# Low parts of the run-ahead chunks by an adding DMA, one-hots in groups of two, and 39 chunks ahead dealt sooner

## The chip, the cores and the metric

The kernel runs on one core of a Trainium2 chip. The metric is the time of one execution on the device in microseconds (us). Before the change three runs gave a median of 1723.9 us (1723.31 to 1724.44). In what follows PE is the matmul engine (TensorE), PEld its weight loads, DVE is VectorE, ACT is ScalarE, POOL is GpSimd, and SP only issues DMAs.

## The reference

One transformer-like layer on 512 tokens of width 1024, in float32. First a token-mixing half (two kinds of attention, gates, projections, a residual add). Then a retrieval half, which is what the change touches:

```
q = rms_norm(x) @ w_q                          # 8 heads, two halves of 128 each
scores = q . sub_keys                          # 128 keys per half
top 16 of each half, sums of pairs, top 16     # -> 16 experts per head, of 128*128
gate = softmax(best)
act = gelu(u[expert] . h)                      # u, v: 16384 experts x 1024
out = x + sum(gate * act * v[expert])
```

An expert's number is 128 times one key index plus another. 8 heads with 16 experts make 128 experts for each token.

## The kernel before

**The dense way.** For three of the four blocks of 128 tokens (`DT`, together 384 tokens) the kernel doesn't gather rows of `u` and `v`. It runs over all 128 *chunks* of 128 experts. For a chunk `first` (L678) computes the products of `u` with all 384 tokens on PE (`pa`) and their gelu (`ga`); the sweep (L799) multiplies `ga` by a gate matrix that is zero where an expert wasn't chosen, and adds its product with the chunk of `v` into `acc`. The fourth block (`GT`) gathers its rows with indirect DMAs from POOL (L762) and multiplies them on DVE, in the background of the sweep.

**Two parts of a float.** PE multiplies a rounded format (`fp32r`). So each operand is split into a high part (rounded) and a low part (the rest), and `mm3` (L145) makes three matmuls: high by high, high by low, low by high. `split` (L668) makes the parts of a chunk in two halves of 128x512: ACT copies to `uh` (L673), and an engine subtracts `uh` from the raw chunk `ut` into `ul` (L674). That engine is POOL for the chunks that run ahead, and DVE in the sweep. Each of `uh` and `ul` has three buffers (`UB`), so three halves are in flight; a chunk is 24 matmuls, 12 for a half.

**Running ahead.** `AHEAD` = 37 chunks of `first` run before the sweep. `more` (L692) deals them out: 2 at once, then one at every third step of `retrieve` (L638, called for the four blocks, 6 steps each), then one for each group of 16 tokens in the gate stage below, and the rest.

**Retrieval.** For each block, `retrieve` turns the chosen places into key indices: ACT copies the places to a one-hot tile `oh` (L646), DVE compares (L647), multiplies by the candidates' indices (L649), and adds up the 16 columns in a tree of four additions of 8, 4, 2 and 1 columns (L651 to L653).

**The gate stage.** For each of 24 groups of 16 tokens (`TB`), DVE builds five tiles of 128x2048 two-byte numbers: one-hots of both key indices (`o1`, `o2`), multiplied by parts of the gate (L738 to L742). In these tiles `TI` = 4 tokens lie side by side: element (key, token) of a group of four stands at 4*key + token. PE multiplies for each token the 128x128 one-hots of both sides, twice (32 matmuls in a group, L747). So the 128 columns that such a matmul reads stand 4 elements, or 8 bytes, apart. ACT copies the result out of PSUM (L750, L751), and SP stores it to DRAM (`spool`).

**Order.** A scheduler puts the instructions of each engine in an order when the program is built; on the chip each engine runs its list in that order and waits at the first that isn't ready. Buffers are released by semaphores when the last reader is done.

Of the kernel before, what the change touches and what calls it, by code (L numbers as in the profile page):

```python
# [8 lines left out]
F32 = mybir.dt.float32  # L9
F32R = mybir.dt.float32r  # L10
# [4 lines left out]
AF = mybir.ActivationFunctionType  # L15
OP = mybir.AluOpType
AX = mybir.AxisListType
# [12 lines left out]
RES = 8  # L30
OCT = 8
TB = 16
TI = 4
AHEAD = 37
S2, GAT, WB, UB, VB = 8, 4, 3, 3, 3
COLS = 3 * 3 * D
PACE = 1.05 * 2 * P * len(GT) / (COLS * (2 * P - AHEAD))
# [10 lines left out]
def block_kernel(ctx, tc, x, mix_gain, w_in, gate_bias, q_gain, k_gain, sinks, w_up_a, w_up_b, w_out,  # L48
                 ffn_gain, w_q, keys_t, peer_u, peer_v, peer_ut, out):
    nc = tc.nc  # L50
# [587 lines left out]
    def retrieve(j):  # L638

        r = NT - 1 - j  # L640
        ia, ib = (gwk.tile([P, HEADS, 16], F32, name=f"{n}{j}") if j in DT else
                  rp.tile([P, HEADS, 16], F32, name=f"{n}{j}") for n in ("ia", "ib"))
        for sel, half, dst in ((a_, 0, ia), (b_, 1, ib)):
            oh = rp.tile([P, HEADS, 16, 16], BF16, name="oh", tag="oh", bufs=2)
            oh2 = oh.rearrange("p h k j -> p (h k) j")
            A.activation(oh2, sel[:, r, :, None].to_broadcast([P, P, 16]), AF.Copy)  # L646
            V.tensor_tensor(out=oh2, in0=oh2, in1=i16[:, None, :].to_broadcast([P, P, 16]), op=OP.is_equal)  # L647
            yield
            V.tensor_tensor(out=oh, in0=oh, in1=idf[:, r, :, half, None, :].to_broadcast([P, HEADS, 16, 16]), op=OP.mult)  # L649
            yield  # L650
            for n in (8, 4, 2):  # L651
                V.tensor_tensor(out=oh[:, :, :, 0:n], in0=oh[:, :, :, 0:n], in1=oh[:, :, :, n:2 * n], op=OP.add)  # L652
            V.tensor_tensor(out=dst, in0=oh[:, :, :, 0], in1=oh[:, :, :, 1], op=OP.add)  # L653
            yield
        KEYS[j] = ia, ib, gate[:, r]
        if j in GT:
            ROWS[j] = gwk.tile([P, HEADS, 16], I32, name=f"ex{j}")
            V.scalar_tensor_tensor(out=ROWS[j], in0=ib, scalar=128.0, in1=ia, op0=OP.mult, op1=OP.add)
# [9 lines left out]
    def split(pool, src, name, eng, bufs):  # L668

        res = []  # L670
        for b in range(2):
            hi, lo = (pool.tile([P, KD // 2, P], F32R, name=name + n, tag=name + n, bufs=bufs) for n in ("h", "l"))
            A.activation(hi, src[:, 4 * b:4 * b + 4], AF.Copy)  # L673
            eng.tensor_tensor(out=lo, in0=src[:, 4 * b:4 * b + 4], in1=hi.bitcast(F32), op=OP.subtract)  # L674
            res.append((hi, lo))
        return res

    def first(i2, eng=G):  # L678

        ut = us.tile([P, KD, P], F32, name="ut", tag="ut", bufs=2)  # L680
        nc.sync.dma_start(ut, peer_ut[i2])
        u = split(us, ut, "u", eng, UB)
        pa = pa_.tile([P, 512], F32, name="pa", tag="pa")
        for k in range(KD):
            mm3(pa[:, :T], u[k // 4], h2T, (SL, k % 4, SL), (SL, k, slice(0, T)), k == 0, k == KD - 1)
        ga = upool.tile([P, T], F32, name="ga", tag="ga", bufs=AHEAD)
        A.activation(ga, pa[:, :T], AF.Gelu)
        return ga
# [3 lines left out]
    def more(n):  # L692
        for i2 in range(len(ahead), min(len(ahead) + n, AHEAD)):
            ahead[i2] = first(i2)

    more(2)
    for j in DT + GT:
        for i, _ in enumerate(retrieve(j)):
            if i % 3 == 0:
                more(1)  # L700
    ret.close()

# [1 line left out]
    with ExitStack() as st:  # L704
        bw = scope(st, "bw")
        pg = scope(st, "pg", 4, space=PSUM)
        rep = bw.tile([P, P, TI], F16, name="rep")
        G.iota(rep, pattern=[[1, P], [0, TI]], base=0, channel_multiplier=0, allow_small_or_imprecise_dtypes=True)
        oh = [P, TB // TI, P, TI]
        keys = rep[:, None].to_broadcast(oh)  # L710

        def spread(t):
            return t.rearrange("p (q i) -> p q i", i=TI)[:, :, None, :].to_broadcast(oh)

        for j in DT:
            pt = pg.tile([P, 4, P], F32, name="pg", tag="pg")
            for i in range(3):
                nc.tensor.transpose(pt[:, i, :], KEYS[j][i].rearrange("p h k -> p (h k)"), ident)
            sel = bw.tile([P, 2, P], F16, name="sel", tag="sel")
            A.activation(sel, pt[:, 0:2, :], AF.Copy)  # L720

            part = bw.tile([P, 2, P], F16, name="part", tag="part")
            two, man = (bw.tile([P, P], F32, name=n, tag=n) for n in ("two", "man"))
            power = bw.tile([P, P], BF16, name="power", tag="power")
            V.tensor_scalar(two.bitcast(I32), pt[:, 2, :].bitcast(I32), 0x7F800000, None, op0=OP.bitwise_and)
            V.tensor_scalar(man.bitcast(I32), pt[:, 2, :].bitcast(I32), 0x007FFFFF, 0x3F800000, op0=OP.bitwise_and,
                            op1=OP.bitwise_or)
            V.tensor_copy(power, two)
            V.tensor_copy(part[:, 0, :], man)
            V.tensor_tensor(out=part[:, 1, :], in0=man, in1=part[:, 0, :], op=OP.subtract)  # L730
            for tb in range(P // TB):
                tg = (NT - 1 - j) * (P // TB) + tb
                ts = slice(tb * TB, (tb + 1) * TB)
                stage = bw.tile([P, SP, TB], F32, name="stage", tag="stage", bufs=2)
                o1 = bw.tile(oh, BF16, name="o1", tag="o1", bufs=2)
                o2 = bw.tile(oh, F16, name="o2", tag="o2", bufs=2)
                ow = bw.tile([P, 2, *oh[1:]], F16, name="ow", tag="ow", bufs=2)
                V.tensor_tensor(out=o2, in0=keys, in1=spread(sel[:, 1, ts]), op=OP.is_equal)  # L738
                for i in range(2):
                    V.tensor_tensor(out=ow[:, i], in0=o2, in1=spread(part[:, i, ts]), op=OP.mult)  # L740
                V.tensor_tensor(out=o1, in0=keys, in1=spread(sel[:, 0, ts]), op=OP.is_equal)
                V.tensor_tensor(out=o1, in0=o1, in1=spread(power[:, ts]), op=OP.mult)  # L742
                for q in range(TB // TI):
                    pp = pg.tile([P, TI, P], F32, name="pg", tag="pg")
                    for i in range(TI):
                        for s in range(2):
                            nc.tensor.matmul(pp[:, i, :], lhsT=o1[:, q, :, i], rhs=ow[:, s, q, :, i],  # L747
                                             start=(s == 0), stop=(s == 1))
                    c0 = tg * TB + 4 * q
                    A.activation(gres[:, :, c0:c0 + 4], pp[:, :, 0:RES].rearrange("p t i -> p i t"), AF.Copy)  # L750
                    A.activation(stage[:, :, 4 * q:4 * q + 4], pp[:, :, RES:P].rearrange("p t i -> p i t"), AF.Copy)  # L751
                more(1)
                nc.sync.dma_start(spool[:, :, tg].rearrange("o p i t -> p o i t"),
                                  stage.rearrange("p (o i) t -> p o i t", i=OCT))
# [44 lines left out]
    for i2 in range(P):  # L799
        ga = ahead.pop(i2)  # L800
        vt = vpool.tile([P, KD, P], F32, name="vt", tag="vt", bufs=3)
        nc.sync.dma_start(vt.rearrange("p k n -> p (k n)"), peer_v[i2 * P:(i2 + 1) * P, :])
        v = [[t.rearrange("p k n -> p (k n)") for t in half] for half in split(vpool, vt, "v", V, VB)]
        if i2 >= RES and (i2 - RES) % OCT == 0:
            gs = vpool.tile([P, T // TB, OCT, TB], F32, name="gs", tag="gs")
            nc.sync.dma_start(gs, spool[(i2 - RES) // OCT])
        wh = vpool.tile([P, T], F32R, name="wh", tag="wh")
        wl = vpool.tile([P, T], F32R, name="wl", tag="wl")
        if i2 < RES:
            V.tensor_tensor(out=ga, in0=ga, in1=gres[:, i2, :], op=OP.mult)  # L810
        else:
            g3 = ga.rearrange("p (b t) -> p b t", t=TB)
            V.tensor_tensor(out=g3, in0=g3, in1=gs[:, :, (i2 - RES) % OCT, :], op=OP.mult)
        A.activation(wh, ga, AF.Copy)
        V.tensor_tensor(out=wl, in0=ga, in1=wh.bitcast(F32), op=OP.subtract)
        if i2 + AHEAD < P:
            ahead[i2 + AHEAD] = first(i2 + AHEAD, V)
        for b in range(2):
            for j in DT:
                mm3(acc[j][:, 512 * b:512 * b + 512], (wh, wl), v[b], (SL, cols(NT - 1 - j)), (SL, SL), i2 == 0, i2 == P - 1)  # L820
# [44 lines left out]
```

## Time and profile before

| | |
|---|---|
| median of 3 runs | 1723.9 us |
| the profiled execution: time, span | 1720.6 us, 1718.9 us |
| PE busy | 1651.5 us, 96% of the span |
| DVE, ACT, POOL busy | 75%, 43%, 34% |
| first `pa`, first gate matmul, first `acc`, last `acc` start | 510.6, 604.6, 810.9, 1711.6 us |

The span runs from the first to the last instruction; 1.7 us of the profiled time lie around it. A matmul's duration includes its way through the array, and matmuls overlap; so PE's rate is read from the distance of two starts, not from durations, and a busy share of 96% is not 96% of what PE can do.

### The profile page before, as it was taken

To read this page: it belongs to the slowest core of one execution; us is meant where nothing else is said; L and a number is where in the kernel's file an instruction comes from. 1 tells how busy PE (TensorE), PEld (TensorE's weight loads), DVE (VectorE), ACT (ScalarE), POOL (GpSimd) and SP (SyncE) were. 2 spreads that over 40 slices of the span, in tenths; PEclk is the share of its full clock that TensorE was granted. 3 is DMA by queue.
4 is the path that set the end of the run, shared out by engine and by line. 5 is a ranking of instruction groups with operands and counts; after the bars stand their busy time and mean duration, and the time that the engine had idled before them with its cause. 6 is when DMAs were issued, how large, how long until landed. Compare 5 with 4: busy or idle time off the path is not lost.

```text
span 1718.9 us, 24631 instructions
## 1 busy us (share of the span) xinstructions
PE 1651.5 (96%) x8969; PEld 1466.4 (85%) x8969; DVE 1282.0 (75%) x2471; ACT 745.8 (43%) x1457; POOL 582.7 (34%) x446
## 2 busy tenths in 40 slices
PE   6999999999996899989999999999999999999998
PEld 5887777798885798989999999999999999998886
DVE  5444345635999998898897878777777777877874
ACT  4557635533324454545344343343344434443442
POOL 4100011512323654453343434334444343433310
PEclk9999999999998899999999999999999999999999
DMA  4321231123301364657999988888988888877874
GB/s 159 98 75 50 73 89 59 62 87 125 108 1 62 107 205 145 208 171 244 406 372 344 323 277 314 319 290 318 322 281 313 316 295 310 290 269 248 294 234 145
DMA packets 158347, 361.29 MB, mean 210 GB/s; under 512 B 10385, under 2 KB 86161, under 8 KB 156305
## 3 DMA queue, kind: packets, MB, share of 16 engines
q1 hardware_dynamic: 120496, 224.94, 37.5%
q0 software_dynamic: 36864, 134.23, 23.5%
q8 instruction: 70, 1.15, 0.3%
q10 hardware_dynamic: 864, 0.54, 0.1%
q14 instruction: 53, 0.43, 0.1%
HBM read 331.89 MB, written 27.26 MB: 209 GB/s over the span
## 4 chain that ended last, share of the span: by engine, by line
PE 81%; DVE 13%; issue 3%; ACT 1%; POOL 1%; DMA 0%; DVEq 0%; SPq 0%; ACTq 0%; POOLq 0%
PE acc L148 10%; PE acc L150 10%; PE acc L149 10%; PE pa L148 9%; PE pa L150 9%; PE pa L149 9%; PE pg L747 5%; PE mm L149 5%; PE mm L150 5%; PE mm L148 5%; DVE tt L566 1%; PE z L462 1%; DVE oh L652 1%; PE mm L490 1%; DVE idx L568 1%
## 5 line engine op out<-in xcount | busy, mean ns | idle before, releaser
L148 PE MATMUL pa<-h2Th,uh 128*128 128x384 f32 x1024 | 349.3, 341 | 17.6 <-ACT uh L673 17.2
L150 PE MATMUL pa<-h2Th,ul 128*128 128x384 f32 x1024 | 349.6, 341 | 6.8 <-POOL ul L674 6.8
L149 PE MATMUL pa<-h2Tl,uh 128*128 128x384 f32 x1024 | 348.3, 340 | 0.0
L673 ACT ACTIVATE uh<-ut 128x512 fp32r<-128x512 f32 x256 | 160.9, 632 | 323.4 <-PE pa L149 237.1
L148 PE MATMUL acc<-vh,wh 128*128 128x512 f32 x768 | 301.1, 392 | 0.0
L150 PE MATMUL acc<-vh,wl 128*128 128x512 f32 x768 | 299.9, 390 | 0.0
L149 PE MATMUL acc<-vl,wh 128*128 128x512 f32 x768 | 298.6, 389 | 0.0
L762 POOL DMA_INDIRECT row<-peer_u,ex x128 | 175.2, 1369 | 250.0 <-DVE row L774 193.8
L762 POOL DMA_INDIRECT row<-peer_v,ex x128 | 166.5, 1301 | 267.4 <-DVE xg L784 193.0
L673 ACT ACTIVATE vh<-vt 128x512 fp32r<-128x512 f32 x256 | 159.8, 624 | 140.3 <-PE acc L150 136.5
L148 PEld LDWEIGHTS pa<-h2Th,uh 128*128 128x128 f32 x1024 | 195.6, 191 | 23.5 <-ACT uh L673 19.0
L150 PEld LDWEIGHTS pa<-h2Th,ul 128*128 128x128 f32 x1024 | 195.3, 191 | 8.8 <-POOL ul L674 8.8
L149 PEld LDWEIGHTS pa<-h2Tl,uh 128*128 128x128 f32 x1024 | 195.3, 191 | 3.7
L674 POOL TENSOR_TENSOR ul<-ut,uh 128x512 fp32r<-128x512 f32 x74 | 137.0, 1860 | 172.4 <-ACT uh L673 165.4
L674 DVE TENSOR_TENSOR vl<-vt,vh 128x512 fp32r<-128x512 f32 x256 | 176.6, 690 | 23.5 <-ACT vh L673 22.0
L674 DVE TENSOR_TENSOR ul<-ut,uh 128x512 fp32r<-128x512 f32 x182 | 125.5, 690 | 85.4 <-ACT uh L673 85.4
L150 PEld LDWEIGHTS acc<-vh,wl 128*128 128x128 f32 x768 | 144.1, 188 | 32.5
L149 PEld LDWEIGHTS acc<-vl,wh 128*128 128x128 f32 x768 | 144.2, 188 | 27.3
L148 PEld LDWEIGHTS acc<-vh,wh 128*128 128x128 f32 x768 | 144.2, 188 | 26.3
L784 DVE SCALAR_TENSOR_TENSOR xg<-row,wt,xg 128x1024 f32<-128x1024 f32 x128 | 163.7, 1279 | 1.3
L774 DVE SCALAR_TENSOR_TENSOR row<-row,h 128x1024 f32<-128x1024 f32 x128 | 151.4, 1219 | 4.8 <-DMA row<-peer_u,ex 4.7
L158 DVE TENSOR_TENSOR wlo<-w,whi 128x1024 fp32r<-128x1024 f32 x52 | 64.9, 1250 | 85.9 <-ACT whi L157 81.7
(232 smaller groups left out, 2823.5 us busy)
## 6 DMA issues: line engine op xcount, KB each, us to landing
ut<-peer_ut SPq DMA_DIRECT2D x128, 512.0 KB, 4.9
vt<-peer_v SPq DMA_DIRECT2D x128, 512.0 KB, 6.9
spool<-stage SPq DMA_DIRECT2D x24, 960.0 KB, 5.0
gs<-spool SPq DMA_DIRECT2D x15, 1536.0 KB, 9.7
w<-w_in SPq DMA_DIRECT2D x17, 1024.0 KB, 5.4
w<-w_q SPq DMA_DIRECT2D x8, 1024.0 KB, 5.6
w<-w_out SPq DMA_DIRECT2D x4, 1024.0 KB, 5.1
x<-x SPq DMA_DIRECT2D x4, 512.0 KB, 5.8
```

What stands on the lines that cost most here:

```text
L148: nc.tensor.matmul(ps, lhsT=l[0][li], rhs=r[0][ri], start=start, stop=False)
L149: nc.tensor.matmul(ps, lhsT=l[0][li], rhs=r[1][ri], start=False, stop=False)
L150: nc.tensor.matmul(ps, lhsT=l[1][li], rhs=r[0][ri], start=False, stop=stop)
L158: eng.tensor_tensor(out=lo, in0=raw, in1=hi.bitcast(F32), op=OP.subtract))
L462: nc.tensor.matmul(z[:, :nk], lhsT=qT[:, h, cols(NT - 1 - j)], rhs=kbT[:, h // 2, row0(j):S], start=True, stop=True)
L490: nc.tensor.matmul(PY[j][s * 64:(s + 1) * 64, h // 2, :], lhsT=vb[:, NT - 1 - j + b, h * DH:(h + 1) * DH], rhs=lt[:, b, :], start=(b == 0) ...
L673: A.activation(hi, src[:, 4 * b:4 * b + 4], AF.Copy)
L674: eng.tensor_tensor(out=lo, in0=src[:, 4 * b:4 * b + 4], in1=hi.bitcast(F32), op=OP.subtract)
L747: nc.tensor.matmul(pp[:, i, :], lhsT=o1[:, q, :, i], rhs=ow[:, s, q, :, i], start=(s == 0), stop=(s == 1))
L762: G.indirect_dma_start(out=t, out_offset=None, in_=src, in_offset=bass.IndirectOffsetOnAxis(ap=ex[:, h, k:k + 1], axis=0))
L774: V.scalar_tensor_tensor(out=t, in0=t, scalar=1.0, in1=h2, op0=OP.mult, op1=OP.mult, accum_out=wt[:, h, k:k + 1]))
L784: V.scalar_tensor_tensor(out=xj, in0=t, scalar=wt[:, h, k:k + 1], in1=xj, op0=OP.mult, op1=OP.add))
```

## The change

The low part of a run-ahead chunk is made in another way (`split_dma`): ACT first writes minus the rounded chunk into `ul`, then POOL issues a DMA that reads the same half chunk from DRAM again and adds it on to `ul`; ACT then writes `uh` as before. The chunks that are made in the sweep keep the subtraction on DVE. `TI` becomes 2, with the group of four tokens in PSUM kept. `AHEAD` becomes 39; 5 chunks are dealt at once, and one at every second step of `retrieve`. The tree of four additions in `retrieve` becomes one `tensor_reduce`.

```diff
-TI = 4
-AHEAD = 37
+TI = 2
+AHEAD = 39
@@ retrieve
-            for n in (8, 4, 2):
-                V.tensor_tensor(out=oh[:, :, :, 0:n], in0=oh[:, :, :, 0:n], in1=oh[:, :, :, n:2 * n], op=OP.add)
-            V.tensor_tensor(out=dst, in0=oh[:, :, :, 0], in1=oh[:, :, :, 1], op=OP.add)
+            V.tensor_reduce(out=dst, in_=oh, axis=AX.X, op=OP.add)
@@ new
+    def split_dma(pool, src, raw, name, bufs):
+
+        res = []
+        for b in range(2):
+            hi, lo = (pool.tile([P, KD // 2, P], F32R, name=name + n, tag=name + n, bufs=bufs) for n in ("h", "l"))
+            k = slice(4 * b, 4 * b + 4)
+            A.activation(lo, src[:, k], AF.Copy, scale=-1.0)
+            G.dma_start(lo, raw[:, k], accum_op=OP.add)
+            A.activation(hi, src[:, k], AF.Copy)
+            res.append((hi, lo))
+        return res
@@ first
-        u = split(us, ut, "u", eng, UB)
+        u = split(us, ut, "u", V, UB) if sweep else split_dma(us, ut, peer_ut[i2], "u", UB)
@@
-    more(2)
+    more(5)
     for j in DT + GT:
         for i, _ in enumerate(retrieve(j)):
-            if i % 3 == 0:
+            if i % 2 == 0:
                 more(1)
@@ gate stage
-                for q in range(TB // TI):
-                    pp = pg.tile([P, TI, P], F32, name="pg", tag="pg")
-                    for i in range(TI):
+                for q in range(TB // 4):
+                    pp = pg.tile([P, 4, P], F32, name="pg", tag="pg")
+                    for i in range(4):
+                        t, k = divmod(4 * q + i, TI)
                         for s in range(2):
-                            nc.tensor.matmul(pp[:, i, :], lhsT=o1[:, q, :, i], rhs=ow[:, s, q, :, i],
+                            nc.tensor.matmul(pp[:, i, :], lhsT=o1[:, t, :, k], rhs=ow[:, s, t, :, k],
                                              start=(s == 0), stop=(s == 1))
```

What the scheduler makes of it on POOL, from the run-ahead chunks on. Before (`ul` the low parts, `wlo` low parts of the weights of w_q, `row` the first gathers of the sweep):

```order
L158 TENSOR_TENSOR wlo<-w,whi 128x1024 x13
L674 TENSOR_TENSOR ul<-ut,uh 128x512 x21
L708 IOTA rep 128x512
L674 TENSOR_TENSOR ul<-ut,uh 128x512
L762 DMA row<-peer_u,ex_5512 128x1024
L674 TENSOR_TENSOR ul<-ut,uh 128x512
```

And after it:

```order
L158 TENSOR_TENSOR wlo<-w,whi 128x1024 x13
L683 DMA ul<-peer_ut 128x512 x23
L718 IOTA rep 128x256
L773 DMA row<-peer_u,ex_5781 128x1024
L683 DMA ul<-peer_ut 128x512
L773 DMA row<-peer_u,ex_5781 128x1024
L683 DMA ul<-peer_ut 128x512 x2
```

POOL's 74 subtractions become 78 DMA issues in the same places of its list; it has no other work between the last `wlo` and the gathers.

On ACT, in the stretch in which `retrieve` runs; `oh` are the copies that `retrieve` needs, `ga` the gelu of a chunk. Before:

```order
L646 ACTIVATE oh<-b__5053 128x2048
L687 ACTIVATE ga<-pa 128x384
L673 ACTIVATE uh<-ut 128x512 x3
L646 ACTIVATE oh<-a__5052 128x2048
L687 ACTIVATE ga<-pa 128x384
L646 ACTIVATE oh<-b__5053 128x2048
```

And after it:

```order
L646 ACTIVATE oh<-b__5053 128x2048
L682 ACTIVATE ul<-ut 128x512
L684 ACTIVATE uh<-ut 128x512
L646 ACTIVATE oh<-a__5052 128x2048
L697 ACTIVATE ga<-pa 128x384
L682 ACTIVATE ul<-ut 128x512
L684 ACTIVATE uh<-ut 128x512
L682 ACTIVATE ul<-ut 128x512
L684 ACTIVATE uh<-ut 128x512
L646 ACTIVATE oh<-b__5053 128x2048
```

The negated copy stands ahead of the high part of the same half, and one or two halves now stand between two `oh` copies. On PE's list 318 `pa` matmuls (13 1/4 chunks) stand ahead of the first gate matmul before the change, and 408 (17 chunks) after it.

In the gate stage, one round on ACT between the evictions of two groups. Before:

```order
L750 ACTIVATE gres<-pg 128x8x4
L751 ACTIVATE stage<-pg 128x120x4
L673 ACTIVATE uh<-ut 128x512
L687 ACTIVATE ga<-pa 128x384
L673 ACTIVATE uh<-ut 128x512
L750 ACTIVATE gres<-pg 128x8x4
```

And after it:

```order
L761 ACTIVATE gres<-pg 128x8x4
L762 ACTIVATE stage<-pg 128x120x4
L682 ACTIVATE ul<-ut 128x512
L684 ACTIVATE uh<-ut 128x512
L682 ACTIVATE ul<-ut 128x512
L684 ACTIVATE uh<-ut 128x512
L697 ACTIVATE ga<-pa 128x384
L761 ACTIVATE gres<-pg 128x8x4
```

Both halves of a chunk are now made between two evictions, so the DMAs of a chunk can't be issued before the last eviction of the group ahead; PE's list has one group of 32 gate matmuls and one chunk in turn.

## Rows read from the trace of the kernel before

**Rows 1.** Page: busy us and instructions; engines in the chain that ended last
```profile
PE 1651.5 (96%) x8969; PEld 1466.4 (85%) x8969; DVE 1282.0 (75%) x2471; ACT 745.8 (43%) x1457; POOL 582.7 (34%) x446
...
PE 81%; DVE 13%; issue 3%; ACT 1%; POOL 1%; DMA 0%; DVEq 0%; SPq 0%; ACTq 0%; POOLq 0%
```
**Rows 2.** Busy time by stage: stretch, its length, engines, clock, DMA share, GB/s
```profile
511.00:605.00 94.00, 66.10 (x325) 61.47 (x324) 91.11 (x230) 40.01 (x53) 50.10 (x30) 0.85 0.27 84
605.00:811.00 206.00, 196.70 (x1367) 191.63 (x1366) 185.34 (x142) 104.37 (x270) 93.56 (x49) 0.95 0.63 189
811.00:1557.00 746.00, 746.00 (x3783) 679.25 (x3782) 602.14 (x928) 296.99 (x550) 300.74 (x223) 1.00 0.88 315
1557.00:1712.00 155.00, 154.96 (x684) 127.97 (x682) 106.00 (x143) 61.62 (x110) 31.75 (x28) 1.00 0.70 231
```
**Rows 3.** First and last start us, by tile: pa, gate matmuls, acc (durations ns min/median/max)
```profile
L148 PE MATMUL pa<-h2Th,uh x1024: 335/336/686, 510.6 to 1556.2; 128*128 128x384 f32 x171
...
L747 PEld LDWEIGHTS <-o x768: 111/117/138, 604.6 to 797.3; 128*128 128x128 bf16 x192
L747 PE MATMUL pg<-ow,o x768: 287/297/303, 604.6 to 797.4; 128*128 128x128 f16 x192
...
L150 PE MATMUL acc<-vh,wl x768: 388/389/397, 811.4 to 1711.6; 128*128 128x512 f32 x192
```
**Rows 4.** Waits from 605 to 811 us: who, for whom, us, times, longest
```profile
PE pg L747 <- DVE o L742: 9.3, 2, 5.3
```
**Rows 5.** Timeline of PE: start us, us; 384 columns first and last of 20, then a gate block
```profile
631.61 0.34 PE L148 MATMUL pa<-h2Th,uh 128*128 128x384 f32 x1
...
634.90 0.34 PE L149 MATMUL pa<-h2Tl,uh 128*128 128x384 f32 x1
635.08 3.95 PE L747 MATMUL pg<-ow,o 128*128 128x128 f16 x32
```
**Rows 6.** Timeline of PE with 256 columns, first and last of 7, and their weight loads
```profile
366.26 0.28 PE L150 MATMUL mm<-whi,mgl 128*128 128x256 f32 x1
...
366.98 0.28 PE L150 MATMUL mm<-whi,mgl 128*128 128x256 f32 x1
...
366.26 0.19 PEld L148 LDWEIGHTS mm<-whi,mgh 128*128 128x128 f32 x1
```
**Rows 7.** Timeline of PE: eight transposes in a row
```profile
395.90 1.04 PE L549 MATMUL tp<-ident,h 128*128 128x128 f32 x8
```
**Rows 8.** A 2048-element build on DVE, alone and beside a subtraction on POOL
```profile
L738 DVE TENSOR_TENSOR o<-rep,sel x24: 1206/1210/2279, 594.2 to 783.5; 128x2048 f16<-128x2048 f16 x24
...
640.87 4.21 POOL L674 TENSOR_TENSOR ul<-ut,uh 128x512 fp32r<-128x512 f32 x2 [3.66 <-ACT uh L673]
...
641.62 2.32 DVE L740 TENSOR_TENSOR ow<-o,part 128x2048 f16<-128x2048 f16 x1
```
**Rows 9.** The tree's narrow steps (timeline), and a reduction over 512 elements
```profile
563.53 0.42 DVE L653 TENSOR_TENSOR ia<-oh 128x128 f32<-128x128 bf16 x1
563.87 0.44 DVE L652 TENSOR_TENSOR oh<-oh 128x256 bf16<-128x256 bf16 x1
...
L614 DVE TENSOR_REDUCE gsum<-gate x1: 677/677/677, 536.7 to 536.7; 128x32 f32<-128x512 f32 x1
```
**Rows 10.** ACT: copies and evictions, 605 to 811 us (mean ns); retrieval's copy
```profile
L751 ACT ACTIVATE stage<-pg 128x480 f32<-128x480 f32 x96 | 54.4, 567 | 0.0
L673 ACT ACTIVATE uh<-ut 128x512 fp32r<-128x512 f32 x48 | 30.4, 633 | 43.2 <-PE pa L149 28.0 <-issue 8.1 <-POOL ul L674 4.5
L750 ACT ACTIVATE gres<-pg 128x32 f32<-128x32 f32 x96 | 18.9, 197 | 57.6 <-PE pg L747 57.5
L687 ACT ACTIVATE ga<-pa 128x384 f32<-128x384 f32 x24 | 11.4, 476 | 0.0
...
L646 ACT ACTIVATE oh<-b__5053 x4: 1898/1899/1902, 541.8 to 579.9; 128x2048 bf16<-128x2048 bf16 x4
```
**Rows 11.** POOL's gathers of 512 KB, 585 to 830 us: issue ns, and landing
```profile
L762 POOL DMA_INDIRECT row<-peer_u,ex x11: 933/1678/1967, 593.9 to 825.6; - x11
...
DMA to landing us min/median/max: 4.4/6.6/11.9
```

More of the change, by code (lines that the diff above doesn't have):

```diff
@@ L676, in split, with first @@
         return res
-    def first(i2, eng=G):
+    def split_dma(pool, src, raw, name, bufs):
[8 more added lines that the diff above has]
+        return res
+    def first(i2, sweep=False):
         ut = us.tile([P, KD, P], F32, name="ut", tag="ut", bufs=2)
         nc.sync.dma_start(ut, peer_ut[i2])
-        u = split(us, ut, "u", eng, UB)
+        u = split(us, ut, "u", V, UB) if sweep else split_dma(us, ut, peer_ut[i2], "u", UB)
         pa = pa_.tile([P, 512], F32, name="pa", tag="pa")
@@ L816, in block_kernel @@
         if i2 + AHEAD < P:
-            ahead[i2 + AHEAD] = first(i2 + AHEAD, V)
+            ahead[i2 + AHEAD] = first(i2 + AHEAD, True)
         for b in range(2):
```

## The prediction

> **What bounds the kernel now.** I read the page's busy shares and its chain first [rows 1]: PE is busy 96% of the span and holds 81% of the chain, DVE 13%. Such a share hides pace, so I went on to the busy time by stage [rows 2]. The reader is to see there three stages. From 811 us on, in the sweep, PE is busy all of 746 us and all but 0.04 us of the last 155: what PE has to do there is all that counts. From 605 to 811, the gate stage, PE is idle for 206 - 196.7 = 9.3 us, all of it two waits for the one-hot builds [rows 4]. From 511 to 605, the retrieval, PE is busy for 66 of 94 us, at a mean granted clock of 0.85 of 2.4 GHz: the only hole of any size. The first and last starts [rows 3] give the frame: first chunk 510.6, first gate matmul 604.6, last `acc` matmul 1711.6.
>
> So there are two ways to win: PE work put into the hole, and PE work made shorter. Moving a chunk from the sweep to before it is worth nothing in itself, since PE does the same 128 chunks; two more chunks ahead count only where they stand in the hole.
>
> **PE's prices.** Starts, not durations. Twenty matmuls of 384 columns start from 631.61 to 634.90 [rows 5]: 3.29/19 = 173 ns each, so a half of 12 is 2.08 us and a chunk of 24 is 4.15 us. Seven of 256 columns start 0.72 us apart from first to last [rows 6]: 120 ns. 128 columns more thus cost 53 ns, and 128 columns alone would cost 120 - 53 = 67 ns. The gate block has 32 matmuls of 128 columns in 3.95 us; less one duration of 0.297 us, that is 3.65/31 = 118 ns [rows 3, 5], nearly twice 67. It isn't the weight loads: those of 0.19 us follow each other every 120 ns in rows 6, and the gate block's take 0.117 us [rows 3]. What sets the gate matmuls apart is that their columns stand 8 bytes apart in SBUF.
>
> **The change part by part.**
>
> *TI = 2.* The columns stand 4 bytes apart, as in the fp32r matmuls that run at full pace. Bounds: 118 ns (no gain) and 67 ns. I take 67, the price that the contiguous rows give: 768 x 51 ns = -39.2 us. On DVE the builds keep their 2048 elements; one alone takes 1.21 us [rows 8]. Their second operand now repeats pairs instead of fours. Bounds are 1.21 us and the 2.32 us that the same build takes beside POOL; I take 1.21, as a pair still is one 4-byte word, and price the other end as a rival.
>
> A rule speaks against the gain: the Trainium skill's page "SBUF — State Buffer", section "Door 1: The DMA port swizzle", says that SBUF is read in 16-byte lines and that two hits in a line are enough for full bandwidth. At 8 bytes a line has two hits, so by that rule nothing is gained here; the sum would be 1721 (first rival). The 118 ns of rows 5 against 67 speak against it, unless something else makes them slow.
>
> *Low parts by DMA.* It removes 74 subtractions on POOL. Beside them a build takes up to 2.32 us in place of 1.21 [rows 8], and DVE is busy 185 of 206 us in the gate stage [rows 2]. Without them five builds cost 5 x 1.21 = 6.05 us a group, 145 us in 24 groups. It adds on ACT 78 copies of 0.633 us (the negated parts), and on POOL 78 DMA issues. A group with a chunk then has on ACT 4 x (0.197 + 0.567) + 4 x 0.633 + 0.476 = 6.06 us [rows 10]: beside PE's work, if a round is longer than that. What matters is the time L from POOL's issue to the landing, because `ul` has three buffers. The trace has no adding DMA. Nearest are the gathers of 512 KB from the same queue: landing 4.4 us at least, 6.6 in the median, 11.9 at most [rows 11]. The new DMA writes half of that, but reads both the source and what it adds to. I take L = 5.0, near the gathers' lower end, for the bytes; the ends I keep are 3.7 (an estimate: the 4.4 less an issue's difference and half the transfer) and 11.9.
>
> The Trainium skill's page "DMA: Bandwidth & Descriptors", section "Anatomy of one DMA — SWDGE (gpsimd) path", has 2.0 us plus the bytes over 436 GB/s, about 2.6 us for 256 KB; it says nothing of adding. By it the sum would be about 1654.
>
> *The hole with 17 chunks.* On PE's list 17 chunks stand ahead of the first gate matmul, 13 1/4 before. A buffer's round is: half chunk 2.08, negated copy 0.63, DMA 5.0, three hand-overs about 0.4 = 8.1 us, for three halves at a time. Three halves are made early, and the last of 34 is the first of the twelfth round: 510.6 + 11 x 8.1 + 2.08 = 601.8. The eight copies of 1.9 us that `retrieve` needs [rows 10] now stand among these copies on ACT; I add all, 15.2 us: 617. So the first gate matmul comes 617 - 604.6 = 12.4 us later, with 3.75 chunks more done, 15.6 us of PE. Queued behind a `ul` that waits for its buffer are, on ACT, those copies (DVE waits for them) and gelus; on POOL only further low parts. DVE's builds for the first group are there by 604.6, as before, so PE's queue is what is late.
>
> *`tensor_reduce`* takes 0.677 us for 512 elements [rows 9], so at most 2.7 us for 2048, eight times 21.7 us, in place of trees whose narrow steps alone take 0.42 to 0.44 us each, and more beside POOL. It is hidden: at 617 PE is still at its chunks. Without that cover it would be worth a few us either way.
>
> *The gate stage.* 22 chunks are left for 24 groups. PE alone needs 4.15 + 32 x 0.067 = 6.29 us a round. But a chunk's DMA is now issued after the last eviction of the group ahead, and PE then has one chunk and one group to do before it needs the result. Two rounds so take 4.15 + 2.14 + the eviction (0.38 + 0.57) + 0.63 + 0.4 + 5.0 = 13.3 us, 6.64 a round: 22 x 0.35 = 7.6 us of new idle time. (Three of these are sums of rows 5 and 10; 0.4 again are hand-overs.) The two waits where a token block ends I leave at 9.3.
>
> Sum: +12.4 - 15.6 - 39.2 + 7.6 = -34.8 us. The profiled execution took 1720.6 (span 1718.9), the median is 3.3 higher; the difference goes on to the median: 1723.9 - 34.8 = **1689 us**. One us of L is worth 34/3 + 22/2 = 22.3 us, so the forecast falls to nothing at L = 6.6.
>
> **The rivals.**
>
> *Gate matmuls keep their pace.* Eight transposes of 128 columns start (1.04 - 0.287)/7 = 108 ns apart [rows 7], so pairs of a weight load and a short matmul may have a floor of their own, and the lines' rule above says so too. Then +39.2, and the new idle time goes (a round of PE is 7.93, the DMA's 7.5): -34.8 + 39.2 - 7.6 = -3.2, 1721; with 108 ns some 1713. Against it: 67 ns from three widths' line.
>
> *The adding DMA is slow.* It reads twice, and the stage's DMA share is 0.63 already [rows 2]. From L = 6.6 on the change costs: at 8 us 3 x 22.3 = 67 more, 1756; at the gathers' 11.9, 1843. Place: PE waits for `ul` in both stages.
>
> *Pairs slow DVE down.* In the tree, a step that reads 128 runs of 2 takes 0.44 us, no less than one of 128 single elements [rows 9], as if each run cost two cycles. If that holds for repeated pairs, a build takes 2.32 us (2.25 from start to start): 24 x 5 x 2.25 = 270 us. With builds from 582 on (retrieval ends earlier without POOL beside it) and 9.3 us at the block ends, the last gate matmul comes near 861 rather than 617 + 22 x 6.64 + 2 x 2.14 + 9.3 = 777: +84, 1773. Against it: those runs lie 32 bytes apart, the pairs repeat one word.
>
> **How the numbers follow.** Forecast 0.57 (L from 3.7 to 6.5; its own range 1660 to 1722). Pace kept 0.18: 1713 to 1727, of which 0.08 faster, 0.07 within, 0.03 slower. Slow DMA 0.14, all slower. Slow builds 0.11, slower. This kernel's runs tell 0.2% (3.4 us) from no change. Faster 0.57 + 0.08 = 0.65, within 0.07, slower 0.03 + 0.14 + 0.11 = 0.28. The range runs from 1660 (L = 3.7) to 1752 (L = 7.8), which leaves out the slow builds and the slowest DMAs, some 0.18.
>
> **What would show it.** Gate matmuls 67 ns apart right, 118 wrong. Landing of `ul` near 5 us. First gate matmul near 617, its last near 777. Builds at 1.21 us throughout; at 2.3 the third rival. PE waiting for `ul`, in the retrieval and some in the gate stage; if for `o1`, DVE is the bound. The sweep from its first `acc` on must be as long a chunk as before, 746 us at full busy time; if it isn't, the forecast is wrong in a place that I left out.

## The result, and the profile after

The changed kernel took 1747.8 us (median; 1746.5 to 1749.3), the kernel before 1723.6 beside it: a ratio of 1.0144 (95% interval 1.0127 to 1.0162). That is 24 us slower where 35 us faster was forecast. The profiled execution has a span of 1747.6 us. Starts, in us:

| | before | after | forecast |
|---|---|---|---|
| first `pa` | 510.6 | 512.2 | 510.6 |
| first gate matmul | 604.6 | 633.0 | 617 |
| last gate matmul | 797.4 | 835.7 | 777 |
| first `acc` | 810.9 | 852.5 | |
| last `acc` | 1711.6 | 1740.8 | |

The tiles' rows of the profile after, as [rows 3] (durations in ns, then first and last start):

```profile
L148 PE MATMUL pa<-h2Th,uh x1024: 335/336/689, 512.2 to 1577.2; 128*128 128x384 f32 x171
...
L758 PE MATMUL pg<-ow,o x768: 217/218/330, 633.0 to 835.7; 128*128 128x128 f16 x192
...
L150 PE MATMUL acc<-vh,wl x768: 388/389/433, 855.8 to 1740.8; 128*128 128x512 f32 x192
```

The stages, as [rows 2] (stretch, length, busy us of PE, PEld, DVE, ACT, POOL; clock, DMA share, GB/s):

```profile
512.20:633.00 120.80, 86.00 (x414) 78.94 (x412) 79.61 (x213) 63.31 (x96) 37.08 (x38) 0.89 0.72 157
633.00:836.00 203.00, 163.45 (x1316) 153.54 (x1315) 128.79 (x123) 112.93 (x302) 36.58 (x43) 0.89 0.92 223
836.00:852.50 16.50, 9.12 (x45) 8.80 (x45) 12.00 (x22) 5.97 (x13) 8.30 (x7) 0.79 1.03 372
852.50:1740.80 888.30, 888.30 (x4385) 794.89 (x4384) 699.56 (x1058) 354.71 (x646) 335.13 (x245) 1.00 0.84 300
```

The sweep is as full as it was, and 12.4 us shorter (888.3 us from first to last `acc`, 900.7 before), as more chunks stand ahead of it. All of the loss lies ahead of it: in the gate stage PE is idle for 39.6 us (9.3 before), at a mean clock of 0.89 (0.95 before), and the DMA engines are in use for 0.92 of the time (0.63 before).

What PE waits for from 511 to 870 us: first after, then before.

```profile
PE pa L150 <- DMA ul<-peer_ut: 64.6, 29, 5.5
PE pa L148 <- ACT ga L697: 9.4, 5, 7.4
PE pa L148 <- ACT uh L684: 5.0, 1, 5.0
```

```profile
PE pa L148 <- ACT uh L673: 17.2, 5, 10.2
PE pg L747 <- DVE o L742: 12.8, 3, 5.3
PE pa L150 <- POOL ul L674: 6.8, 6, 1.5
```

The wait for the builds is gone and one for the adding DMA has come, 29 times. Its landing, in the retrieval and then in the gate stage:

```profile
DMA to landing us min/median/max: 3.8/5.4/8.3
...
DMA to landing us min/median/max: 3.6/7.0/9.5
```

And a wait has a second price. PE's timeline after, behind one wait, with the granted clock of two stretches:

```profile
645.14 0.69 PE L150 MATMUL pa<-h2Th,ul 128*128 128x384 f32 x1 [3.25 <-DMA ul<-peer_ut]
645.62 0.52 PE L148 MATMUL pa<-h2Th,uh 128*128 128x384 f32 x1
645.94 0.52 PE L149 MATMUL pa<-h2Tl,uh 128*128 128x384 f32 x1
...
651.63 0.34 PE L150 MATMUL pa<-h2Th,ul 128*128 128x384 f32 x1
...
657.89 2.01 PE L758 MATMUL pg<-ow,o 128*128 128x128 f16 x32
```

```profile
645.60:651.10 5.50, 5.50 (x19) 5.50 (x19) 1.69 (x2) 1.15 (x2) 0.86 (x1) 0.50 0.94 244
651.80:663.60 11.80, 8.50 (x91) 8.03 (x90) 9.43 (x9) 8.60 (x24) 2.59 (x3) 1.00 0.83 199
```

After 3.25 us of waiting the matmuls of 384 columns start 0.32 us apart in place of 0.173, at a granted clock of 0.50, the lower level of 1.2 GHz, for 5.5 us. Not every wait is followed by such a stretch: of these 29, some 14 are. Over the whole span the mean clocks are 0.974 and, before, 0.984:

```profile
core 0: 1747.6 us, clock 0.974
```

```profile
core 0: 1718.9 us, clock 0.984
```

So (1 - 0.974) x 2 x 1747.6 = 91 us went by at the lower level, 55 before. The last row of the timeline shows the gain that did come: a group of 32 gate matmuls takes 2.01 us, (2.01 - 0.218)/31 = 58 ns from start to start, where it was 118 [rows 5].

The balance from the first `pa` to the last `acc` (1201.0 before, 1228.6 after: +27.6). PE's idle time, the lengths less the busy times of the stage rows, went from 37 to 82 us, +45. The gate matmuls give 768 x 60 ns = -46. *Slower starts* are the other price: where a matmul waited for nothing and yet came later than at its full pace (0.173 us for `pa`, 0.058 for a gate matmul), the excess is counted from the starts in the trace. For `pa` it was 11.9 us in all and is 30.8, +19; for the gate matmuls +4. That makes +22; some 6 us are left unassigned.

### The profile page after: what moved, and what is told of

It reads as the page before. It is cut to its first block, busy times and chain, and to the rows that moved or that the text cites. A ratio compares the mean times of both kernels' runs of the same rounds, so it can differ in the third digit from the quotient of the medians.

```text
span 1747.6 us, 24727 instructions
## 1 busy us (share of the span) xinstructions
PE 1636.8 (94%) x8969; PEld 1443.7 (83%) x8969; DVE 1217.6 (70%) x2443; ACT 781.2 (45%) x1535; POOL 522.8 (30%) x450
## 4 chain that ended last, share of the span: by engine, by line
PE 81%; DMA 9%; issue 6%; DVE 2%; POOL 1%; ACT 1%; DVEq 0%; POOLq 0%; ACTq 0%
PE acc L148 10%; PE acc L150 10%; PE acc L149 10%; PE pa L150 9%; PE pa L148 8%; PE pa L149 8%; DMA ul<-peer_ut 8%; PE mm L149 6%; PE mm L150 6%; PE mm L148 6%; PE z L462 1%; PE mm L490 1%; PE pg L758 1%; PE tp L592 1%; PE z L395 1%
## 5 line engine op out<-in xcount | busy, mean ns | idle before, releaser
L150 PE MATMUL pa<-h2Th,ul 128*128 128x384 f32 x1024 | 359.0, 351 | 66.9 <-DMA ul<-peer_ut 64.6
L148 PE MATMUL pa<-h2Th,uh 128*128 128x384 f32 x1024 | 356.7, 348 | 14.4 <-ACT ga L697 9.4
L149 PE MATMUL pa<-h2Tl,uh 128*128 128x384 f32 x1024 | 354.9, 347 | 0.0
L150 PEld LDWEIGHTS pa<-h2Th,ul 128*128 128x128 f32 x1024 | 200.5, 196 | 77.9 <-DMA ul<-peer_ut 75.5
L773 POOL DMA_INDIRECT row<-peer_v,ex x128 | 175.7, 1373 | 253.0 <-DVE xg L795 183.7
L671 ACT ACTIVATE uh<-ut 128x512 fp32r<-128x512 f32 x178 | 112.6, 633 | 246.3 <-PE pa L149 204.7
L148 PEld LDWEIGHTS pa<-h2Th,uh 128*128 128x128 f32 x1024 | 200.8, 196 | 20.0 <-ACT ga L697 11.2
L149 PEld LDWEIGHTS pa<-h2Tl,uh 128*128 128x128 f32 x1024 | 200.4, 196 | 3.5
L683 POOL DMA_DIRECT2D ul<-peer_ut x78 | 68.3, 883 | 248.9 <-ACT ul L682 225.1
L825 ACT ACTIVATE wh<-ga 128x384 fp32r<-128x384 f32 x128 | 67.1, 525 | 141.2 <-PE acc L149 141.2
```

What stands on the lines that cost most here:

```text
L148: nc.tensor.matmul(ps, lhsT=l[0][li], rhs=r[0][ri], start=start, stop=False)
L149: nc.tensor.matmul(ps, lhsT=l[0][li], rhs=r[1][ri], start=False, stop=False)
L150: nc.tensor.matmul(ps, lhsT=l[1][li], rhs=r[0][ri], start=False, stop=stop)
L683: G.dma_start(lo, raw[:, k], accum_op=OP.add)
L773: G.indirect_dma_start(out=t, out_offset=None, in_=src, in_offset=bass.IndirectOffsetOnAxis(ap=ex[:, h, k:k + 1], axis=0))
```

## The experiments

Ratios are to the kernel before, run on the same chip in the same rounds, with their 95% intervals. "Sooner" is the dealing of the changed kernel (5 at once, every second step). e7 and e12 have the tree, the others `tensor_reduce`; e2 and e3 leave out the true low parts of the run-ahead chunks, so only their times count.

| low parts by | `TI` | dealt, `AHEAD` | us | ratio |
|---|---|---|---|---|
| POOL | 2 | before, 37 (e7) | 1721.6 | 0.9991 (0.9980 to 1.0001) |
| POOL | 2 | sooner, 39 (e1) | 1726.2 | 1.0020 (1.0005 to 1.0036) |
| adding DMA | 4 | before, 37 (e12) | 1761.2 | 1.0223 (1.0196 to 1.0249) |
| adding DMA | 4 | sooner, 39 (e4) | 1761.2 | 1.0228 (1.0211 to 1.0245) |
| adding DMA | 2 | before, 37 (e8) | 1734.5 | 1.0062 (1.0041 to 1.0082) |
| adding DMA | 2 | sooner, 39 (the change) | 1747.8 | 1.0144 (1.0127 to 1.0162) |
| plain DMA | 2 | sooner, 39 (e3) | 1711.4 | 0.9931 (0.9910 to 0.9953) |
| no DMA | 2 | sooner, 39 (e2) | 1660.4 | 0.9647 (0.9631 to 0.9663) |
| adding DMA, 4 `ul` | 2 | sooner, 38 (e5) | 1707.7 | 0.9907 (0.9886 to 0.9927) |
| adding DMA, 6 `ul` | 2 | sooner, 35 (e6) | 1727.9 | 1.0022 (1.0011 to 1.0033) |
| adding DMA, 4 `ul` | 2 | before, 38 (e11) | 1706.4 | 0.9908 (0.9883 to 0.9933) |

### Is it the DMA? (e2, e1)

e2 takes it away:

```diff
             A.activation(lo, src[:, k], AF.Copy, scale=-1.0)
-            G.dma_start(lo, raw[:, k], accum_op=OP.add)
```

> The changed kernel without the adding DMA: ul keeps minus the rounded chunk, so the low parts of the run-ahead chunks are not the reference's; all else stays. Theory A (landing of the DMA plus the half clock behind each wait is the whole loss): no wait for ul, gate stage bound by builds of 1.22 us (24 x 6.1 = 146 us and some waits where a block ends), first gate matmul near 607, last near 762, first acc near 775, time 1670 (1660 to 1685). Theory B (ACT's extra copies or the sooner dealing hold PE up as well): PE waits for uh or ul on ACT, time 1700 or more.

1660.4 us: theory A, at the lower end of its range. First gate matmul 603.7, last 745.3, and in the gate stage PE is busy 136 of 142 us at a clock of 0.99; DVE is nearly as full, 134.8:

```profile
603.70:746.00 142.30, 136.45 (x1266) 129.31 (x1267) 134.76 (x129) 107.26 (x293) 0.70 (x1) 0.99 0.79 231
```

So the DMA alone costs 87 us, and everything else in the change is worth 62 (against the 1722.3 of the kernel before beside it) if the low parts cost nothing but ACT's copies. From the first `pa` to the last `acc` PE is idle for 24 us in e2 and for 82 with the DMA, and its slower starts take 9 us in e2 and 35 with it: 57 us are waits, 26 the lower clock. The kernel with the same parts and POOL's subtraction is e1:

```diff
-        u = split(us, ut, "u", V, UB) if sweep else split_dma(us, ut, peer_ut[i2], "u", UB)
+        u = split(us, ut, "u", V if sweep else G, UB)
```

> The changed kernel with the run-ahead low parts made by POOL's subtraction again (hi copy on ACT, low part on POOL); TI = 2, AHEAD = 39, the sooner dealing and tensor_reduce stay. Theory A (the adding DMA costs: its landing of 5.4 to 7.0 us makes PE wait for ul, and PE runs at the half clock after each wait): the waits for ul go, first gate matmul near 607, then the builds beside POOL bound the gate stage as before (DVE busy 185 us of it), last gate matmul near 800, first acc near 810, time 1705 (1690 to 1715). Theory B (dealing sooner or TI = 2 is what costs): time stays at 1735 or more.

1726.2: neither theory's time. No wait for a DMA is left, but the 62 us are gone too. PE's waits:

```profile
PE pg L758 <- DVE o L752: 26.4, 8, 5.6
PE pa L150 <- POOL ul L672: 24.5, 9, 6.7
```

The gate stage came as expected (191 us), the retrieval did not: first gate matmul at 620.7 in place of 607, as the subtractions of 19 chunks beside it now slow retrieval down: DVE is busy for 88.9 us of it, in e2 for 72.8 with the same 208 instructions, and the first build starts at 609.2, in e2 at 596.6. The retrieval's rows, e1 and then e2:

```profile
512.20:620.70 108.50, 87.91 (x466) 83.53 (x465) 88.92 (x208) 49.83 (x71) 66.76 (x43) 0.92 0.34 112
511.60:603.70 92.10, 82.06 (x465) 81.38 (x463) 72.82 (x208) 67.82 (x108) 3.98 (x4) 0.94 0.38 128
```

### How long, and why (e3, e5, e6)

e3 replaces the adding DMA by one that only copies, with every engine's list alike:

```diff
-            G.dma_start(lo, raw[:, k], accum_op=OP.add)
+            G.dma_start(lo, raw[:, k].bitcast(F32R))
```

> The changed kernel with a plain copying DMA in place of the adding one, of the same 256 KB from the same queue, with every engine's list the same; ul then holds the raw chunk, so low parts are not the reference's. Theory A1 (the addition itself makes the landing long): landing falls to about 4 us in the retrieval and in the gate stage, waits for ul mostly go, time 1690 (1675 to 1710). Theory A2 (any DMA from POOL of this size takes that long beside the stage's other DMAs): landing stays at 5.4 and 7.0 us, time 1740 to 1755.

1711.4, 36 us less than with the addition: between the theories, just above A1's range in time, while the landing fell less than A1 said. Worked out from the packets in the trace (from POOL's issue to the end of the last packet), the median landing is 4.1 and 5.7 us, with the addition 5.1 and 6.5. A packet of 2 KB takes 99 ns, an adding one 178. So the addition is worth 1 us of landing and 36 us of time; the rest of the 87, 51 us, is any DMA at this place. 1 us by the forecast's 22.3 us per us is 22. What PE lost shows the remainder: its idle time falls by 19 us (82 to 63), and its slower starts by 16 (35 to 19), with 55 us at the lower level in place of 91.

e5 gives the loop a fourth buffer (the second line stands in `split` and in `split_dma`):

```diff
-AHEAD = 39
+AHEAD = 38
-hi, lo = (pool.tile([P, KD // 2, P], F32R, name=name + n, tag=name + n, bufs=bufs) for n in ("h", "l"))
+hi, lo = (pool.tile([P, KD // 2, P], F32R, name=name + n, tag=name + n, bufs=(bufs if name == "v" else 3 if n == "h" else 4)) for n in ("h", "l"))
```

> The changed kernel with four ul buffers instead of three (uh keeps three) and AHEAD = 38 for the room. On ACT the negated copies, and so the DMA issues behind them, then stand two to three groups ahead of the chunk's place on PE. Theory A (it is the loop through three buffers that lays the landing on PE, and a fourth hides it): PE's waits for ul in all fall from 64.6 to under 15 us, the half-clock stretches go with them, time 1675 (1663 to 1695), near the 1660 measured without the DMA. Theory B (the DMA engines or POOL's queue are full, so the landing grows as more DMAs are in flight): landing of 9 us or more, waits stay, time 1725 or more.

1707.7: between the theories again, and faster than both kernels. The waits for `ul` fall from 64.6 to 28.8 us, but don't go. In the gate stage POOL now issues a DMA 8.9 us (median) before PE gets to its half, 6.8 in the changed kernel, so the fourth buffer bought 2 us. Two things in the trace may stand in the way of more, and neither was tried: the DMA engines are in use for 0.98 of the gate stage, and ACT's negated copies wait for the load of the raw chunk `ut`, which has two buffers. In the changed kernel they never did. PE's and ACT's waits, from 510 and from 512 us on:

```profile
PE pa L150 <- DMA ul<-peer_ut: 28.8, 20, 2.8
...
ACT ul L682 <- DMA ut<-peer_ut: 33.4, 19, 4.4
```

```profile
627.80:792.00 164.20, 139.39 (x1240) 131.85 (x1240) 133.28 (x128) 103.50 (x285) 30.49 (x36) 0.93 0.98 254
```

e6 (six `ul` buffers, `AHEAD` = 35):

> The changed kernel with six ul buffers and AHEAD = 35 for the room. Theory A: no waits for ul left, and what four chunks fewer ahead cost is 4 x 4.15 = 17 us at most, since PE has nothing else in the gate stage: 1675 (1665 to 1690), no better than four buffers. Theory B (four buffers leave waits): 10 us or more below the kernel with four.

1727.9, later than either said. The waits for `ul` halve once more (14.0 us), but 72 `pa` matmuls fewer stand in the gate stage than in e5 (12.5 us, done later in the sweep), and PE waits there for builds instead (17.2 us). The first `pa` is 4 us later too, and ACT's negated copies wait 61.5 us for `ut`. As I read it, a chunk ahead is worth its 4.15 us as long as it covers a wait.

### What the gate matmuls gained (e4, e7)

e4 is the changed kernel with `TI = 4`:

> The changed kernel with one-hots in groups of 4 again; lists of PE, DVE and ACT in the same order. Gate matmuls go from 58 to 118 ns apart, 46 us more work on PE. Theory A (the gate stage is paced by the DMA loop, so most of the gate matmuls' gain is turned into waiting for ul): the waits for ul in the gate stage shrink to under 20 us and the half-clock stretches with them, time 1760 (1750 to 1775). Theory B (the gain of groups of 2 counts in full): waits as long as before, time 1790 or more.

1761.2, theory A (1760). The price is 118 ns again (its block of 32 takes 3.96 us), so it is the distance of the columns, in both operands, that sets it. Of the 46 us only 13 show: against the changed kernel PE's idle time is 20 us less and its slower starts 13 us less. It waits 47.0 us for `ul` in all, and the clock in the gate stage is 0.98.

```profile
PE pa L150 <- DMA ul<-peer_ut: 47.0, 28, 5.5
...
634.20:848.40 214.20, 193.52 (x1313) 183.50 (x1313) 129.88 (x124) 122.06 (x302) 38.10 (x43) 0.98 0.89 213
```

e7 is the kernel before with `TI = 2` alone:

> The kernel before with TI = 2 alone: 37 chunks ahead, dealt as before, low parts by POOL, the tree. Theory A (gate matmuls at 58 ns take 46 us off PE, but the builds beside POOL's subtractions then bound the gate stage, DVE having been busy 185 of 206 us in it): PE waits for o1, gain of 10 to 20 us, 1706 (1700 to 1715). Theory B (with POOL's subtractions the gain of pairs is nothing, as the kernel with POOL's subtractions and the sooner dealing took 1726): 1720 or more. Theory C (counts in full): 1680.

1721.6, theory B: no difference that can be measured. PE waits 35.2 us for builds (12.8 before) which take 2.3 us beside POOL:

```profile
PE pg L748 <- DVE o L742: 35.2, 14, 5.6
```

```profile
640.82 2.31 DVE L738 TENSOR_TENSOR o<-rep,sel 128x2048 f16<-128x2048 f16 x1
643.05 2.28 DVE L742 TENSOR_TENSOR o<-o,power 128x2048 bf16<-128x2048 bf16 x1
645.25 2.35 DVE L740 TENSOR_TENSOR ow<-o,part 128x2048 f16<-128x2048 f16 x2
647.52 1.21 DVE L741 TENSOR_TENSOR o<-rep,sel 128x2048 bf16<-128x2048 f16 x1
```

The third row is two builds in 2.35 us: the slow ones of the forecast's third rival are POOL's doing, not the pairs'. In the changed kernel none takes over 1.23 us.

### Where the chunks stand (e8, e12, e11)

e8 is the changed kernel dealt as before:

```diff
-AHEAD = 39
+AHEAD = 37
-    more(5)
+    more(2)
-            if i % 2 == 0:
+            if i % 3 == 0:
```

> The changed kernel with AHEAD = 37, 2 chunks at once and one at every third step of retrieval; the adding DMA, TI = 2 and tensor_reduce stay. 12.8 chunks instead of 17 stand ahead of the first gate matmul. Theory A (the DMA loop paces PE in both stages, so it matters little where a chunk stands): first gate matmul 26 us earlier, near 607; rounds of the gate stage as long; some three chunks more left behind it and two more in the sweep, 20 us: 1742 (1735 to 1752). Theory B (dealing sooner is itself a loss): 1725 or less. Theory C (dealing sooner gained its 15.6 us): 1760 or more.

1734.5, just under theory A's range, so dealing sooner (with two chunks more ahead) is itself a loss of 13 us here. First gate matmul 612.8 with 12.8 chunks ahead of it, 633.0 with 17: 20.2 us later for 17.3 us of PE's work. PE's idle time in the retrieval is there in both, 30 us in e8 and 35 with 17 chunks, but it is the loop's own waits, and more chunks bring more of them. The gate stage is 12 us shorter too (190.6): 0.8 chunk less (3.5 us), and slower starts of `pa` take 10.5 us in place of 18.3.

e12 is the kernel before with `split_dma` alone, e11 is e5 dealt as before:

> The kernel before with the adding DMA alone: TI = 4, AHEAD = 37, dealt as before, the tree. Theory A (the DMA loop with its half-clock stretches is a loss by itself, and 13 us come from dealing sooner): 1748 (1738 to 1758), 24 us over the kernel before. Theory B (the DMA is harmful only with many chunks in the retrieval): 1730 or less.

> Four ul buffers, AHEAD = 38, all low parts of the run-ahead by the adding DMA, but dealt as before the change: 2 chunks at once and one at every third step of retrieval (13.8 chunks ahead of the first gate matmul in place of 19.1). Theory A (a chunk put among retrieval's work costs as much there as it saves later, as the 13 us of the old dealing with three buffers say): first gate matmul near 608, 1700 (1692 to 1706). Theory B (with four buffers the sooner dealing pays for itself): 1712 or more.

e12 took 1761.2, 13 more than I expected, over theory A's range, and as long as e4: with `TI` = 4 the dealing makes no difference that shows, though e4 also has `tensor_reduce` and two chunks more ahead. e11 took 1706.4, 0.4 over theory A's range and no better than e5: with four buffers, and `AHEAD` alike, it makes none either. The loss by dealing sooner was seen only with three buffers and `TI` = 2; why it needs both isn't settled.

### Half by DMA (e9, e10)

Both start from e5 and make only one half of a chunk by DMA, e9 everywhere, e10 in the gate stage alone. The part of the edit that does it (`eng` is POOL or DVE, and `None` where both halves keep the DMA):

```diff
...
-            A.activation(lo, src[:, k], AF.Copy, scale=-1.0)
-            G.dma_start(lo, raw[:, k], accum_op=OP.add)
+            if b == 0 or eng is None:
+                A.activation(lo, src[:, k], AF.Copy, scale=-1.0)
+                G.dma_start(lo, raw[:, k], accum_op=OP.add)
             A.activation(hi, src[:, k], AF.Copy)
+            if b == 1 and eng is not None:
+                eng.tensor_tensor(out=lo, in0=src[:, k], in1=hi.bitcast(F32), op=OP.subtract)
...
```

> Four ul buffers, AHEAD = 38, the sooner dealing, and only the first half of a run-ahead chunk by the adding DMA; the second half is subtracted, by POOL while retrieval runs and by DVE in the gate stage. Theory A (with four buffers the DMA engines themselves are full in the gate stage: 0.99 of their time there): the landing in the gate stage falls from 6.5 us to about 5, PE's waits for ul by DMA go, and DVE bounds the stage at 24 x (6.1 + 0.69) = 163 us; with some 10 us from the retrieval 1698 (1688 to 1708). Theory B (the landing is a fixed delay): it stays at 6.5 us, and waits for ul of 20 us or more stay: 1708 or more.

> As the kernel with four ul buffers, but in the gate stage alone the second half of a chunk is subtracted by DVE; all of the retrieval's low parts by the adding DMA. Theory A (DMA engines full in the gate stage): landing near 5 us there, DVE bound at 163 us, first gate matmul near 628 as with four buffers: 1706 (1698 to 1713), no gain, since one bound of 164 us gives way to another of 163. Theory B (DMA landing is what four buffers still lacked): 1695 or less.

1727.4 and 1727.5 (1.0037, 1.0024 to 1.0050; 1.0035, 1.0025 to 1.0045). e9 has the time of theory B and the landing of theory A; e10 misses both. In the gate stage the DMA share is 0.77 in e9, and by the packets the landing falls to 4.4 us (e5: 6.6). Yet PE waits longer than in e5, and for the same DMA:

```profile
PE pa L150 <- DMA ul<-peer_ut: 47.8, 26, 6.9
...
622.70:810.00 187.30, 144.57 (x1241) 135.58 (x1242) 148.48 (x149) 97.90 (x270) 16.99 (x20) 0.91 0.77 204
```

ACT's list puts the one negated copy of a chunk late, behind the high parts of the chunk ahead, which wait for their own buffers: in the gate stage POOL issues the DMA 3.0 us (median) before PE gets to that half, less than the 4.4 us of its landing; in e5 the two are 8.9 and 6.6. A shorter landing is no help where the DMA is issued late. That another order would mend it was not tried.

## Why the prediction was wrong, point by point

*What bounds it*: right. The sweep stayed full, and but for 1.6 us ahead of the first `pa` the loss arises from 512 to 852 us.

*TI = 2*: right in the price, and more than taken: 58 ns, not 67, 46 us off PE. e4 shows the price, by itself, and that only 13 us of it reach the time in this loop; the sum had counted all but 7.6 of its 39.2. The rule cited from the Trainium skill's "SBUF — State Buffer", "Door 1: The DMA port swizzle", by which pairs in a line are already enough, isn't borne out by these matmuls: 118 ns at 8 bytes, 58 at 4. That the builds keep their 1.21 us was right too, so the third rival is out (1.22 us, [rows 8] for before).

*Low parts by DMA, L = 5.0*: this term failed in size. The landing was 5.4 us in the retrieval and 7.0 in the gate stage. By the forecast's own sensitivities that is 0.4 x 34/3 + 2.0 x 22/2 = 26.5 us. I had placed L near the lower end of the gathers [rows 11] by its bytes. Two things were in the rows and not in the choice: the stage's DMA share of 0.63 [rows 2], which the new DMA itself drove to 0.92, and the double reading, 178 ns for a packet in place of 99 (e3). The 2.6 us, an estimate by the Trainium skill's page "DMA: Bandwidth & Descriptors", section "Anatomy of one DMA — SWDGE (gpsimd) path", lay below the shortest landing here, 3.6 us.

*The hole with 17 chunks*: the first gate matmul came at 633.0, not 617. Of the 16.0 us, 1.6 are the later first `pa` and 11.1 are slower starts; the 3.3 that are left fit the 4.5 of L. The price of slower starts stood in no term: the sum took PE at 0.173 us a matmul throughout, though the clock of 0.85 in this stage [rows 2] was a sign that PE doesn't run at full pace there.

*The gate stage*: 202.7 us from first to last gate matmul, where the forecast had 160. L makes 22 by the forecast's own sensitivity, slower starts 18.3 + 4.0 = 22 (some 2 of it the first start behind each gate block, at full clock); against it the faster gate matmuls and the build waits that I had left in, 12. Some 11 are unassigned. Sixteen and 43 make 59 us, as much as the miss by the medians (by the profiled spans it is 63.5: 1747.6 against 1718.9 - 34.8). The landing is some 26 of it, the slower starts 33.

*Which step failed*: two terms of the sum. L was mis-sized, 5.0 where 5.4 and 7.0 were measured; with that alone put right the forecast's sum gives 1689 + 26.5 = 1716, still faster than before. The pace of PE was put at 0.173 us throughout, that is, the price of slower starts at nothing; it was 33 us, and it is with this term that the sum turns to slower. That 1747.8 lies inside the stated range, 1660 to 1752, is luck: the range went by L alone and has 1752 at a landing of 7.8. Its lower end was also off by the forecast's own terms: at L = 3.7 the gate stage has only its 7.6 us to give, which makes 1667.

*`tensor_reduce`*: 2.28 us each, within the 2.7 taken; that it is hidden fits the late first gate matmul, and it was not tried alone.

*The rivals*: "slow adding DMA" is what happened, in its place (PE waits for `ul` in both stages). Its break-even of 6.6 us was too high: with the slower starts counted the change lost at a landing of 5.4 and 7.0. It had a chance of 0.14. The price for being wrong, 22 us per us of landing, had been worked out and should have kept the forecast from leaning on the one number no row showed.

## What to carry to other kernels

Work taken off a busy engine and given to a DMA puts the DMA's landing into every loop that waits for it; divide it by the buffers in flight, and give the loop a buffer more before judging the change (here 1747.8 against 1707.7 us). When PE is near full, its waits cost their length and then the lower clock behind some of them, here about half as much again (57 and 26 us for the DMA, 19 and 16 for its addition). And a faster stage is worth only what its next bound leaves: groups of two took 46 us off PE, and that was worth nothing measurable beside POOL's subtractions, 13 us in the DMA loop dealt sooner, 27 in the loop dealt as before (`tensor_reduce` among it).

## What the runs showed of the hardware

- An adding DMA of 128 x 2 KB took 178 ns a packet, a copying one 99; POOL's issue of it took 0.86 us against 0.53.
- f16 matmuls of 128 columns start 58 ns apart with columns 4 bytes apart, 118 ns with 8.
- Behind a wait of 3.25 us PE's granted clock was 0.50 for 5.5 us of dense work. Without the DMA (e2) the mean clock is 0.990, with it 0.974.
- An equality or product of 2048 two-byte elements takes 1.21 to 1.22 us on DVE whether its broadcast operand repeats pairs or fours, and 2.3 us beside a subtraction on POOL in either case (e7, [rows 8]).
